# Letting branches into TensorE's queue only between half jobs of a hybrid decoder layer

## The chip, the cores and the metric

The kernel runs on one core of one Trainium2 chip. The metric is the device time of one execution in microseconds (us). A profiled execution of the same kernel gives the trace. Its engines are TensorE (PE: matrix products, weight loads shown apart as PEld), VectorE (DVE), ScalarE (ACT), GpSimd (POOL) and SyncE (SP, which issues the transfers).

## The reference

One layer over 1024 tokens of width 1024, everything float32. The input is normalised and multiplied by one wide matrix; its columns feed three branches, their gates and a merge.

```python
h = rms_norm(x, norm_g[l])
proj = jnp.einsum('bsd,dn->bsn', h, w_in[l])
(a_val, a_glu, a_gate, b_q, b_f, b_i, b_gate,
 c_q, c_k, c_v, c_gate, c_f, merge) = jnp.split(proj, split_points, axis=-1)
ya = conformer_conv(a_val, a_glu, ...) * jax.nn.silu(a_gate)
yb = hgrn2(b_q, b_f, b_i, ...) * jax.nn.silu(b_gate)
yc = forgetting_attention(c_q, c_k, c_v, c_f + fox_f_bias[l], ...) * jax.nn.silu(c_gate)
branches = jnp.stack([ya, yb, yc], axis=2)
branch_d = jnp.einsum('bskc,kcd->bskd', branches, w_branch[l])
gates = jax.nn.sigmoid(merge.reshape(B, S, N_BRANCH, D_MODEL))
mixed = jnp.sum(gates * branch_d, axis=2)
x = x + jnp.einsum('bsd,de->bse', mixed, w_out[l])
```

Branch a is a causal convolution of width 31 with a layer norm. Branch b is a gated linear recurrence with 8 heads of width 128 (hgrn). Branch c is causal attention with 16 heads of width 64, normalised q and k, and a forget bias.

## The kernel before

**The linear stream.** Every dense product is cut into jobs (138 of them): 128 output columns by 1024 tokens, in two half jobs of 512 tokens. To keep float32 accuracy, operands are split into a high and a low part, and a half job is 8 steps of k with three matmuls each (high x high, high x low, low x high), 24 matmuls of 128x512 into one PSUM bank. `lin` (L359) runs through the jobs in a fixed order. At the start of a job it fetches the weights of the job after next and splits the weights of the next one (`split`, L342): ScalarE copies the high part (whi, L354), VectorE subtracts it (wlo, L355). Raw, high and low weights have two buffers each, so the copy for a job needs the buffer of the job two before. When a half job is done, `j.done` evicts its bank.

**The branches** are generators that share the engines with the stream. Per head pair c (0 to 7) the jobs are q, k, v and gate of attention, then q, f, i and gate of hgrn. As their results come, these start:

- `qkprep` (L478): eight transposes of k (L494), ScalarE squares; two pairs of matmuls with the matrix ones_bd give the mean squares of q, one bank per half (L501). Then Ln (L504, L507), Exp (L508, L510), Square (L516), and VectorE's Newton step that reads both banks (L519) before they are given back.
- `att` and `soft`: four groups of score blocks (Khi, Klo against Qst, one bank each, two ScalarE evictions each), maximum, Exp, sums, then products with V and the row sums with ones64, both with 64 output rows.
- `hgrn` (L711): levels of 2, 8 and 32 tokens. The inner levels are 32 small products with 32 output rows (`inner_level`), level 32 is 24 of them. Then seven transposes of k, seven products KN times V (L843), a chain of seven states, and 15 output products (L859).
- `conv`: 31 VectorE steps for a group of 128 channels, while the stream goes on.

**Who decides the order.** `Sched.run` (L169) holds an estimate of each engine's time. The stream is a generator too: only where it yields can a branch go on. There the run loop resumes each branch that is ready by its estimate, until none is left, and returns to the stream. Branches take their PSUM banks from a pool of five (`bget`, `bput`, L229, L235), the stream has three of its own.

```python
if pick is not None:
    if not self.resume(pick):
        self.cos.remove(pick)
    continue
if linlive and (self.lin.cond is None or self.lin.cond()):
    linlive = self.resume(self.lin)
    continue
```

What the generators issue is the program's order. The framework's scheduler then sets the final order of each engine by priority and by its own clock, and can pull an instruction past others. On the chip each engine's queue runs strictly in that order: a stalled matmul holds up everything behind it.

Of the kernel before, what the change touches and what calls it, by code (L numbers as in the profile page):

```python
# [198 lines left out]
def build(tc, x, norm_g, w_in, conv_w, conv_b, ln_g, ln_b, hgrn_g, f_bias, qn_g, kn_g,  # L199
# [24 lines left out]
    def ps_lin():  # L224

        lbanks.append(lbanks.pop(0))
        return lbanks[-1]
# [70 lines left out]
    def fput(*ts):  # L298
        F.put(*ts)
# [38 lines left out]
    def fetch(j):  # L338
        j.raw = wpool.tile([P, KT, P], F32, name="wraw", tag="wraw", bufs=2)
        nc.sync.dma_start(out=j.raw, in_=j.src.rearrange("(k p) c -> p k c", p=P))  # L340

    def split(j, eng=nc.vector, pin=lambda ins: ins):  # L342
        if j.narrow:
            j.buf = F.get(dt=F32R)
            j.hi = j.buf[:, 0:S].rearrange("p (k c) -> p k c", k=KT)

            pin(nc.scalar.activation(j.hi, j.raw, AF.Copy))
            pin(eng.tensor_tensor(out=j.hi[:, :, 32:48], in0=j.raw[:, :, 0:16],
                                  in1=j.hi[:, :, 0:16].bitcast(F32), op=ALU.subtract))
            return  # L350
        j.hi = wpool.tile([P, KT, P], F32R, name="whi", tag="whi", bufs=2)
        j.lo = wpool.tile([P, KT, P], F32R, name="wlo", tag="wlo", bufs=2)
        with tc.high_priority(0 if sc.lin is None else HP):
            pin(nc.scalar.activation(j.hi, j.raw, AF.Copy))  # L354
            pin(eng.tensor_tensor(out=j.lo, in0=j.raw, in1=j.hi.bitcast(F32), op=ALU.subtract))  # L355
        sc.t["act"] += 950
        sc.t["dve"] += 1240

    def lin(jobs, hooks):  # L359
        seq = [(0, 0), (1, 0), (2, 0), (0, 1), (1, 1), (2, 1)]  # L360
        seq += [(n, h) for n in range(3, len(jobs)) for h in (0, 1)]
        for m, (n, half) in enumerate(seq):
            j = jobs[n]
            for i in {3: (3,), 5: (4,)}.get(m, (n + 2,) if n > 2 and not half else ()):
                if i < len(jobs):
                    fetch(jobs[i])
            for i in {5: (3,)}.get(m, (n + 1,) if n > 2 and not half else ()):
                if i < len(jobs):
                    split(jobs[i])
            if not half and j.pre is not None:  # L370
                yield from j.pre()
            X = j.X()
            ps = ps_lin()
            hs = slice(half * H2, (half + 1) * H2)
            for k in range(KT):
                a, b = X[0][k][:, hs], X[1][k][:, hs]
                sc.mm(ps, j.hi[:, k, :], a, k == 0, False, 228)
                sc.mm(ps, j.hi[:, k, :], b, False, j.narrow and k == KT - 1, 228)
                if not j.narrow:
                    sc.mm(ps, j.lo[:, k, :], a, False, k == KT - 1, 228)  # L380
                if (m, k) in hooks:
                    hooks[m, k]()
                if k == 3:
                    yield 0
            j.done(half, hs, ps)
            if j.narrow and half:
                fput(j.buf)
            yield 0

        yield from odirect()  # L390
# [723 lines left out]
    def odirect():  # L1114
        yield lambda: od.get("ok")
        mh, ml = Y["mix"]
        parts = [(o, min(H2, OW - o)) for o in range(0, OW, H2)]
        for i in range(KT):
            yield need(2)
            xt, ot = F.get(), F.get()  # L1120
            ts_ = slice(i * P, (i + 1) * P)
            nc.sync.dma_start(out=xt[:, 0:OW], in_=x[ts_, OC * P:])
            pss = [ps_lin() for _ in parts]
            for k in range(KT):
                for a, b, first, last in ((mh, "hi", True, False), (mh, "lo", False, False),
                                          (ml, "hi", False, True)):
                    for ps, (o, n) in zip(pss, parts):
                        sc.mm(ps[:, 0:n], a[k][:, ts_], od[b][:, k, o:o + n], first and k == 0,
                              last and k == KT - 1, n * 0.42 + 3)
                if k in (3, 7):  # L1130
                    yield 0
            for ps, (o, n) in zip(pss, parts):
                sc.tt(ot[:, o:o + n], ps[:, 0:n], xt[:, o:o + n], ALU.add)
            nc.sync.dma_start(out=out[ts_, OC * P:], in_=ot[:, 0:OW])
            fput(xt, ot)
# [176 lines left out]

    sc.start(yb(), "yb")
    sc.run(lin(jobs, {(1, 7): lambda: x_two_out(0), (2, 3): lambda: x_two_out(1)}))
    ctx.close()
    return sc
# [29 lines left out]
```

## Time and profile before

| | |
|---|---|
| median of 3 runs | 1905.27 us (1904.55 to 1906.85) |
| profiled execution, its own time | 1904.65 us |
| its span, first to last instruction | 1902.9 us |
| mean granted clock of TensorE | 0.999 |
| busy: TensorE, VectorE, ScalarE, GpSimd | 1885.2, 1285.2, 953.6, 186.2 us |
| attention and hgrn on TensorE | from about 65 to 1062 us |
| linear stream alone on TensorE | from there on |

The profile gives busy time per engine, the groups of instructions, who waited for whom, and a timeline. Matmuls are pipelined, so rows overlap: the time that a matmul takes from the next one is the distance between their starts, not its own length. Rows that say x64 stand for 64 records in a row; a float32 product that is not of the split kind leaves two records (xcount 8 is four products). Time that an engine stood idle ahead of a row is in brackets, with what ended it.

### The profile page before, as it was taken

Reading aid. Unit: us, or ns where it says so; the run is one execution under the profiler, and the core shown is the slowest. Engines: PE = TensorE matmul, PEld = TensorE weight load, DVE = VectorE, ACT = ScalarE, POOL = GpSimd, SP = SyncE. Lnnn points to the kernel's source line nnn. Section 1 sums busy time; section 2 is a strip of 40 time slices with the busy share of each in tenths; the row PEclk is TensorE's granted clock in tenths of the full one; section 3 lists DMA queues with packets and bytes.
Section 4 is the critical chain, followed back from the end, with each engine's and each line's share of the span. In section 5 each row is a group of like instructions: output and inputs, shape, how many; then the busy total and the mean of one; then the engine's idle time right before and its main releaser. Section 6 shows DMA issues by size and latency. Waiting matters only on the chain.

```text
span 1902.9 us, 27032 instructions
## 1 busy us (share of the span) xinstructions
PE 1885.2 (99%) x11075; PEld 1548.8 (81%) x11075; DVE 1285.2 (68%) x1692; ACT 953.6 (50%) x1508; POOL 186.2 (10%) x164
## 2 busy tenths in 40 slices
PE   8999999999999999999999999999999999999999
PEld 6877878878878788787887888888888888888888
DVE  6567595775856857659577999999995467413431
ACT  6777768767687687776875411111221234321210
POOL 2021120211202111112021100000000010000000
PEclk9999999999999999999999999999999999999999
DMA  4111101111111111110111322222444553213431
GB/s 147 48 31 45 56 23 45 56 45 45 34 45 45 34 52 38 45 56 23 45 56 46 133 78 67 78 67 67 134 147 151 194 160 92 85 45 104 118 129 49
DMA packets 173011, 140.82 MB, mean 74 GB/s; under 512 B 4909, under 2 KB 155445, under 8 KB 172888
## 3 DMA queue, kind: packets, MB, share of 16 engines
q1 hardware_dynamic: 172888, 139.10, 23.7%
q8 instruction: 86, 1.41, 0.3%
q14 instruction: 37, 0.30, 0.1%
HBM read 109.72 MB, written 29.36 MB: 73 GB/s over the span
## 4 chain that ended last, share of the span: by engine, by line
PE 85%; ACT 7%; DVE 3%; DMA 3%; issue 1%; SPq 0%; POOL 0%; DVEq 0%; ACTq 0%; POOLq 0%
PE bank L111 84%; ACT fb L124 4%; ACT khi L124 1%; DVE fa L128 1%; PE bank L115 1%; ACT L124 1%; DMA zdram<-fa 1%; ACT fa L124 1%; DVE fb L128 1%; DMA fa<-zdram 1%; DMA fb<-in_hgrn_norm_g_dram 1%; DMA wraw<-in_w_in_dram 0%; ACT whi L354 0%; DVE klo L132 0%; DVE wlo L355 0%
## 5 line engine op out<-in xcount | busy, mean ns | idle before, releaser
L111 PE MATMUL bank<-hT_hi,whi 128*128 128x512 f32 x1792 | 706.8, 394 | 0.0
L111 PE MATMUL bank<-hT_hi,wlo 128*128 128x512 f32 x1792 | 701.3, 391 | 0.8 <-DVE wlo L355 0.8
L111 PE MATMUL bank<-hT_lo,whi 128*128 128x512 f32 x1792 | 701.2, 391 | 0.0
L111 PEld LDWEIGHTS bank<-hT_hi,wlo 128*128 128x128 f32 x1792 | 336.8, 188 | 72.9 <-issue 2.4
L111 PEld LDWEIGHTS bank<-hT_hi,whi 128*128 128x128 f32 x1792 | 337.0, 188 | 69.8 <-issue 3.2
L111 PEld LDWEIGHTS bank<-hT_lo,whi 128*128 128x128 f32 x1792 | 337.3, 188 | 63.8 <-issue 0.2
L354 ACT ACTIVATE whi<-wraw 128x1024 fp32r<-128x1024 f32 x137 | 144.9, 1058 | 356.9 <-PE bank L111 346.9
L132 DVE SCALAR_TENSOR_TENSOR fa<-fa,taps,fa 128x1024 f32<-128x1024 f32 x240 | 300.0, 1304 | 0.4
L355 DVE TENSOR_TENSOR wlo<-wraw,whi 128x1024 fp32r<-128x1024 f32 x137 | 191.8, 1400 | 112.2 <-ACT whi L354 109.9
L128 DVE TENSOR_TENSOR fa<-fa,fa 128x512 f32<-128x512 f32 (+3 forms) x226 | 173.8, 784 | 67.0 <-ACT fa L124 50.4
L124 ACT ACTIVATE fa<-bank 128x512 f32<-128x512 f32 (+2 forms) x182 | 102.5, 572 | 141.7 <-PE bank L111 131.0
L111 PE MATMUL bank<-yhi,whi 128*128 128x512 f32 x384 | 149.4, 389 | 0.0
L111 PE MATMUL bank<-yhi,wlo 128*128 128x512 f32 x384 | 149.2, 389 | 0.0
L111 PE MATMUL bank<-ylo,whi 128*128 128x512 f32 x384 | 149.2, 389 | 0.0
L124 ACT ACTIVATE fb<-bank 128x512 f32<-128x512 f32 (+5 forms) x262 | 114.2, 451 | 40.6 <-PE bank L111 32.1
L128 DVE TENSOR_TENSOR fa<-fa,fb 128x512 f32<-128x512 f32 (+1 forms) x121 | 81.8, 676 | 59.0 <-ACT fb L124 37.8
L124 ACT ACTIVATE fb<-bank,negF,rk 128x256 f32<-128x256 f32 (+1 forms) x184 | 89.2, 549 | 47.7 <-PE bank L111 31.8
L124 ACT ACT_TABLE_LOAD x83 | 106.5, 1283 | 4.5 <-DVE fb L128 3.0
L132 DVE SCALAR_TENSOR_TENSOR fa<-fa,bank 128x512 f32<-128x512 f32 x96 | 65.7, 686 | 60.0 <-PE bank L111 60.0
L124 ACT ACTIVATE fa<-fa 128x256 f32<-128x256 f32 (+3 forms) x109 | 75.9, 721 | 55.3 <-DMA zdram<-fa 29.6
L124 ACT ACTIVATE fb<-fb 128x1024 f32<-128x1024 f32 (+2 forms) x96 | 88.1, 953 | 15.8 <-DVE fb L128 14.8
L111 PEld LDWEIGHTS bank<-yhi,wlo 128*128 128x128 f32 x384 | 72.1, 188 | 15.0
(163 smaller groups left out, 2128.7 us busy)
## 6 DMA issues: line engine op xcount, KB each, us to landing
wraw<-in_w_in_dram SPq DMA_DIRECT2D x113, 512.0 KB, 3.8
wraw<-in_w_branch_dram SPq DMA_DIRECT2D x24, 512.0 KB, 3.9
zdram<-fa SPq DMA_DIRECT2D x16, 512.0 KB, 4.1
mdram<-fa SPq DMA_DIRECT2D x32, 256.0 KB, 2.0
fa<-mdram SPq DMA_DIRECT2D x16, 512.0 KB, 3.8
fa<-zdram SPq DMA_DIRECT2D x16, 512.0 KB, 3.3
fa<-in_x_dram SPq DMA_DIRECT2D x9, 512.0 KB, 5.2
yc<-fb SPq DMA_DIRECT2D x8, 512.0 KB, 2.6
```

The costliest lines, as they stand in the source:

```text
L111: self.nc.tensor.matmul(out, lhsT=lhsT, rhs=rhs, start=start, stop=stop)
L115: self.nc.tensor.transpose(out, in_, ident)
L124: return self.nc.scalar.activation(out, in_, func, **kw)
L128: self.nc.vector.tensor_tensor(out=out, in0=a, in1=b, op=op)
L132: self.nc.vector.scalar_tensor_tensor(out=out, in0=a, scalar=s, in1=b, op0=op0, op1=op1)
L354: pin(nc.scalar.activation(j.hi, j.raw, AF.Copy))
L355: pin(eng.tensor_tensor(out=j.lo, in0=j.raw, in1=j.hi.bitcast(F32), op=ALU.subtract))
```

## The change

`lin` yielded twice in each half job: after the k step 3, that is 12 matmuls, and after the half job is evicted. The first of the two is removed. The two hooks of the start-up, the fetches and the splits stay where they are.

```diff
                     sc.mm(ps, j.lo[:, k, :], a, False, k == KT - 1, 228)
                 if (m, k) in hooks:
                     hooks[m, k]()
-                if k == 3:
-                    yield 0
             j.done(half, hs, ps)
             if j.narrow and half:
                 fput(j.buf)
```

No instruction is added or taken away, so what changes is their order. The rows below are instructions in the order of one engine's queue: line, operation, output <- inputs, shape, xcount. A name like bank4_80 or fa1_154_4395 is a buffer, number and use. Lines behind the removed ones are two lower after the change.

First place: TensorE in the middle of the fifth head pair (c = 4), where attention's last row sums (ones64, 64 output rows) meet an inner level of hgrn (gt0, 32 output rows). Linear matmuls are those with hT. Before:

```order
L111 MATMUL bank2_78<-hT_lo_144,whi_4463 128x512
L111 MATMUL bank5_81<-fa3_147_4258,ones64_86 64x256 x2
L111 MATMUL bank3_79<-fa6_149_4384,fb1_127_3800 64x256 x2
L111 MATMUL bank3_79<-fa6_149_4384,fb1_127_3800 64x128 x2
L111 MATMUL bank2_78<-hT_hi_143,wlo_4464 128x512
L111 MATMUL bank3_79<-fa4_150_4385,ones64_86 64x256 x2
L111 MATMUL bank4_80<-gt0_133,fa9_138_4045 32x48 x32
L111 MATMUL bank2_78<-hT_hi_143,whi_4463 128x512
```

After the change:

```order
L111 MATMUL bank2_78<-hT_hi_143,wlo_4454 128x512
L111 MATMUL bank5_81<-fa9_147_4271,ones64_86 64x256 x2
L111 MATMUL bank4_80<-gt0_133,fa1_138_4033 32x48
L111 MATMUL bank3_79<-fa0_149_4398,fb3_127_3786 64x256 x2
L111 MATMUL bank3_79<-fa0_149_4398,fb3_127_3786 64x128 x2
L111 MATMUL bank4_80<-gt0_133,fa1_138_4033 32x48 x4
L111 MATMUL bank3_79<-fa5_150_4399,ones64_86 64x256 x2
L111 MATMUL bank4_80<-gt0_133,fa1_138_4033 32x48 x27
L111 MATMUL bank0_76<-hT_hi_143,whi_4453 128x512
```

Two groups have become one, with the two kinds of small products interleaved.

Second place: TensorE a little later in the same pair. bank7 before and bank4 after hold the mean square of q's first half (ones_bd). Before, from the first ones_bd to the next use of that bank:

```order
L115 MATMUL bank3_79<-ident_84,fb1_158_4646 128x128 x4
L111 MATMUL bank4_80<-fb0_144_4243,fa1_154_4395 128x128 x2
L111 MATMUL bank7_83<-fb2_159_4804,ones_bd_101 128x512 x2
L111 MATMUL bank4_80<-fb0_144_4243,fa1_154_4395 128x128
...
L111 MATMUL bank1_77<-hT_hi_143,wlo_4763 128x512
L111 MATMUL bank7_83<-fb5_151_4392,fb0_144_4243 128x128
```

After the change, with 10 of the linear matmuls between the first two rows shown, 20 between the two groups of outputs and 3 ahead of the last products left out in part:

```order
L111 MATMUL bank4_80<-fb4_159_4766,ones_bd_101 128x512 x2
...
L111 MATMUL bank2_78<-hT_hi_143,wlo_4643 128x512
L111 MATMUL bank6_82<-fb5_144_4243,fa4_154_4409 128x128 x4
...
L111 MATMUL bank5_81<-fb0_160_4769,ones_bd_101 128x512 x2
...
L115 MATMUL bank6_82<-ident_84,fb4_161_4850 128x128 x4
L111 MATMUL bank1_77<-hT_hi_143,whi_4762 128x512
L111 MATMUL bank1_77<-hT_lo_144,whi_4762 128x512
L111 MATMUL bank1_77<-hT_hi_143,wlo_4763 128x512
L111 MATMUL bank4_80<-fb5_144_4243,fa4_154_4409 128x128 x3
```

KN times V (fb5, fa4) was 4, 2 and 1 products ahead of and around the first ones_bd; now four come after it, and the last three use its bank again.

Third place: ScalarE over the same stretch. fb1_158 before and fb6_158 after hold k, then the Ln of q's mean square. Before:

```order
L124 ACTIVATE fb1_158_4646<-bank3_79 128x512
L124 ACT_TABLE_LOAD
L124 ACTIVATE sm_119<-sm_119,eps_t_93 128x16
L124 ACTIVATE fb1_158_4646<-bank7_83,eps_t_93 128x512
L124 ACT_TABLE_LOAD
L124 ACTIVATE rk_118<-sm_119 128x16
L354 ACTIVATE whi_4918<-wraw_4760 128x1024
L124 ACT_TABLE_LOAD
L124 ACTIVATE fb1_158_4646<-bank3_79,eps_t_93 128x512
```

After the change:

```order
L124 ACTIVATE fb6_158_4646<-bank5_81 128x512
L354 ACTIVATE whi_4918<-wraw_4760 128x1024
L124 ACT_TABLE_LOAD
L124 ACTIVATE sm_119<-sm_119,eps_t_93 128x16
L124 ACTIVATE fb6_158_4646<-bank4_80,eps_t_93 128x512
L124 ACTIVATE fb4_161_4850<-bank2_78 128x512
L124 ACTIVATE fa2_152_4407<-bank6_82 128x128
L124 ACT_TABLE_LOAD
L124 ACTIVATE rk_118<-sm_119 128x16
L124 ACT_TABLE_LOAD
L124 ACTIVATE fb6_158_4646<-bank5_81,eps_t_93 128x512
```

The weight copy whi has moved from behind the first half's Ln to ahead of the table load for it.

## Rows read from the trace of the kernel before

**Rows 1.** The page's first part, the whole span: busy us (share) xinstructions.
```profile
PE 1885.2 (99%) x11075; PEld 1548.8 (81%) x11075; DVE 1285.2 (68%) x1692; ACT 953.6 (50%) x1508; POOL 186.2 (10%) x164
```
**Rows 2.** Timeline of TensorE from 560 us: start us, us, instruction.
```profile
560.98 0.62 PE L111 MATMUL bank<-fb,ones_bd 128*128 128x512 f32 x2
561.45 0.40 PE L111 MATMUL bank<-hT_hi,wlo 128*128 128x512 f32 x1
...
564.19 0.39 PE L111 MATMUL bank<-hT_hi,wlo 128*128 128x512 f32 x1
...
570.51 0.38 PE L111 MATMUL bank<-fb,fb 128*128 128x128 f32 x2
...
572.29 0.60 PE L115 MATMUL bank<-ident,fb 128*128 128x128 f32 x4
572.65 0.48 PE L111 MATMUL bank<-hT_hi,whi 128*128 128x512 f32 x1
```
**Rows 3.** Timeline of TensorE at 634 us: row sums alone between linear matmuls.
```profile
633.85 0.39 PE L111 MATMUL bank<-hT_hi,wlo 128*128 128x512 f32 x1
634.17 0.65 PE L111 MATMUL bank<-fa,ones 128*64 128x256 f32 x4
...
635.09 0.39 PE L111 MATMUL bank<-hT_lo,whi 128*128 128x512 f32 x1
```
**Rows 4.** Timeline of TensorE at 519 us: an inner level alone.
```profile
518.65 0.39 PE L111 MATMUL bank<-hT_hi,wlo 128*128 128x512 f32 x1
518.97 0.89 PE L111 MATMUL bank<-gt,fa 128*32 128x48 f32 x64
...
520.13 0.40 PE L111 MATMUL bank<-hT_lo,whi 128*128 128x512 f32 x1
```
**Rows 5.** Timeline of TensorE at 534 us: row sums and an inner level together.
```profile
533.78 0.50 PE L111 MATMUL bank<-hT_hi,wlo 128*128 128x512 f32 x1
534.22 0.65 PE L111 MATMUL bank<-fa,ones 128*64 128x256 f32 x4
534.80 0.89 PE L111 MATMUL bank<-gt,fa 128*32 128x48 f32 x64
...
535.95 0.40 PE L111 MATMUL bank<-hT_lo,whi 128*128 128x512 f32 x1
```
**Rows 6.** Timeline of TensorE at 553 us: KN times V, transposes of k.
```profile
552.17 0.40 PE L111 MATMUL bank<-hT_hi,whi 128*128 128x512 f32 x1
552.83 1.16 PE L111 MATMUL bank<-fb,fa 128*128 128x128 f32 x8 [0.26 <-ACT fa L124]
...
554.98 0.40 PE L111 MATMUL bank<-hT_hi,whi 128*128 128x512 f32 x1
555.65 0.66 PE L115 MATMUL bank<-ident,fb 128*128 128x128 f32 x4 [0.28 <-ACT fb L124]
```
**Rows 7.** Waits, whole span: who waited for whom, us in total, times, longest.
```profile
ACT whi L354 <- PE bank L111: 346.9, 79, 9.8
```
**Rows 8.** Timeline of ScalarE from 559 us: qkprep's Ln and Exp, a weight copy.
```profile
559.44 0.31 ACT L124 ACTIVATE sm<-sm,eps_t 128x16 f32<-128x16 f32 x1 [0.52 <-DVE sm L497]
559.66 0.67 ACT L124 ACTIVATE fb<-bank,eps_t 128x512 f32<-128x512 f32 x1
560.34 1.28 ACT L124 ACT_TABLE_LOAD   x1
...
561.76 1.05 ACT L354 ACTIVATE whi<-wraw 128x1024 fp32r<-128x1024 f32 x1
562.83 1.28 ACT L124 ACT_TABLE_LOAD   x1
564.12 0.69 ACT L124 ACTIVATE fb<-bank,eps_t 128x512 f32<-128x512 f32 x1
...
566.61 2.15 ACT L124 ACTIVATE fb<-fb 128x1024 f32<-128x1024 f32 x2
```
**Rows 9.** Timeline of VectorE at 569 us: the Newton step reads the two banks.
```profile
568.79 1.29 DVE L132 SCALAR_TENSOR_TENSOR fb<-bank,fb 128x512 f32<-128x512 f32 x2 [4.73 <-ACT fb L124]
```

## The prediction

> **What bounds the kernel now.** I read the page's busy times first: TensorE works for 99% of the span, VectorE for 68%, ScalarE for half [rows 1]. So only three things can move the time: what TensorE's own instructions cost in another order, a stall of TensorE, and a stall that goes. The number of matmuls is the same in both kernels (9538, counted in the two orders of instructions).
>
> The timeline of TensorE comes next. A linear matmul follows the one ahead of it after 0.228 us (twelve of them between the two linear rows of 2.74 us [rows 2]), whatever its own row says of its length. A branch's group is therefore priced from the start of the linear matmul ahead of it to the start of the second one behind it, less two such steps. Four matmuls of the row sums (64-row outputs) alone: 1.24 - 0.46 = 0.78 us [rows 3]. 64 matmuls of an inner level (32-row outputs) alone: 1.48 - 0.46 = 1.02 us [rows 4]. Both in one group: 2.17 - 0.46 = 1.71 us, of which 0.12 us is a wait (its first matmul starts 0.44 us after the linear one, 0.32 us where the same group stood alone) [rows 3, 5]. So 1.59 us without the wait, and the fusion saved 0.78 + 1.02 - 1.59 = 0.21 us. Fused, the engine changes the height of its output tile three times (128 to 64 to 32 to 128) in place of four: **one change of tile height costs 0.21 us** of TensorE.
>
> The same timeline shows the stalls that repeat in each of the seven later head pairs: KN times V starts 0.66 us after the linear matmul ahead of it (0.43 us too late), the second four transposes of k 0.67 us (0.44 us too late) [rows 6], the row sums 0.12 us as above. That is 0.99 us per pair, and each ends with a ScalarE or VectorE row whose work began when a linear job ended.
>
> **What the change does.** It takes away the scheduler's chance to let branches in after the 12th matmul of a half job. Branches wait for the end of the half job, more of them are ready there, and they go in together. SyncE moves the same transfers and GpSimd does the same work; a transfer or a table step shifts by a fraction of a job (10.9 us), and the weights are prefetched a whole job ahead, so I cost that at nothing: the two weight buffers hide it. If they did not, VectorE's split of a weight tile would come late and TensorE would wait for it.
>
> *Tile heights.* Counted over TensorE's whole order, the height of the output changes 169 times before and 207 times after: 38 more, although the number of branch groups barely moves (240 and 238). The first place in the order shows how: five changes became seven, because inner-level matmuls and row sums that now enter together are interleaved. Per head pair 21 became 26. Cost: 38 x 0.21 = **+8.0 us**. From below nothing excludes that a change straight from 64 to 32 rows is cheaper in other mixes; from above the row gives 0.21 plus perhaps its 0.12 us wait. I take 0.21, a row of just this mixture.
>
> *Stalls that go.* In the new order KN times V comes 24 linear matmuls after the last of the transposes that it needs (2 before), the first transposes of k leave with level 32, and the second come 38 linear matmuls after k's end (31 before). The row sums lead a group 21 linear matmuls behind the one ahead of it (1 before). 7 x 0.99 = **-6.9 us**; the bounds are none of it and all of it, and I take all, since the distances grew by several us against waits below half a us.
>
> *A stall that comes.* The second and third place in the order show it. The last three KN-times-V products (L843) now go into the bank of the first half of q's mean square (bank4). Before, the next to use those banks were the outputs of chunks 4 to 7 (L859), later in the queue. The bank is free only when VectorE has read it for the Newton step (L519). VectorE there needs Square, Exp and Ln of ScalarE. Before, ScalarE loaded the Ln table and finished the first half's Ln ahead of the next weight copy (whi). Now the weight copy stands first in ScalarE's queue, and that copy waits until TensorE has finished the job two before it (its buffer is one of two; these copies wait for TensorE 79 times, 346.9 us in all [rows 7]).
>
> So both engines start at the same moment: the end of v's job. ScalarE's leg, from its rows of before [rows 8]: from the start of whi to VectorE's read 568.79 - 561.76 = 7.03 us; now behind whi come also a table load (1.29), the small Ln with the first half's Ln (560.34 - 559.44 = 0.90), and the load with rk (561.76 - 560.34 = 1.42). Sum 10.64 us, then half of VectorE's pair, 0.65 us [rows 9]: **11.3 us** until the bank is free. Two short copies that also moved into this leg I leave out; they would add 0.1 or 0.2.
>
> TensorE's leg over the same stretch, in the order of the change: four products at 0.22 (eight of them in 1.78 us), 4 linear, the two matmuls of ones_bd (0.47), 20 linear, three products, eight transposes (four in 0.36), 3 linear [rows 2]: 0.89 + 0.91 + 0.47 + 4.56 + 0.67 + 0.72 + 0.68 = **8.9 us**. TensorE arrives 2.4 us early and stalls, with every linear matmul queued behind it: linear jobs, whose inputs are ready, cannot pass. The pattern stands in each pair from the second to the eighth: 7 x 2.4 = **+16.8 us**. Before, the same bank was free at about 569.4 (half of VectorE's pair) and used at 570.51: 1.1 us of slack [rows 2, 9], so no stall. Bounds: none, if ScalarE gets through 2.4 us sooner than its rows of before; 3.4 us, if each hand-over between the engines adds what the waits above show (0.4 us twice or so). I take 2.4.
>
> The Trainium skill (ScalarE: Activation LUTs, What ACT_TABLE_LOAD costs) counts 1.38 us of draining on top of each load, 2.66 us in all. The rows show none here: the load at 562.83 is followed by the next activation 1.29 us later [rows 8].
>
> *What else is late.* Five banks serve all branches; the attention's clusters of five blocks (now two in a row, 22 linear matmuls apart) need their banks evicted by ScalarE in between, 22 x 0.228 = 5.0 us. No row prices that; I take nothing and leave it to the third rival.
>
> Sum: 8.0 - 6.9 + 16.8 = +17.9 us on the profiled execution's 1904.65 us, so 1922.5 us. The median of the runs shown is 0.6 us above that execution; I leave the difference out. About 0.2% (3.8 us) is what a measurement of this kernel can tell from no change.
>
> **The rivals.**
> 1. The bank is free in time. Same switches, same stalls gone: 8.0 - 6.9 = +1.1, 1905.8 us, no change. It decides at ScalarE: if its leg is 8.9 us instead of 11.3, for instance because the weight copy starts sooner or a table load is missing. Against it: the new order still has all four loads in this leg, and the copy's buffer comes free only with the job's last use of it. Chance 0.10.
> 2. Faster: no bank stall, and the changes between 64 and 32 rows (30 of the 38 extra ones) cost nothing: 8 x 0.21 - 6.9 = -5.2, 1899.4 us. Against it: rows 5 is such a change, and it paid. Chance 0.05.
> 3. More stalls than one. The new order leaves more single linear matmuls between groups (38, before 23), places where the framework's scheduler thought a branch not ready yet. If three more of them per pair wait 0.43 us as KN did, 7 x 3 x 0.43 = +9.0: 1931.5 us. Chance 0.08.
> 4. Table loads with the skill's draining: four loads lengthen ScalarE's leg by an amount that no row shows. Chance 0.01.
>
> By the page's figure (an estimate from ScalarE: Activation LUTs of the Trainium skill) rival 4 would be 4 x 1.38 = 5.5 us more per pair, some 1961 us.
>
> **How the numbers follow.** The forecast has 0.76. Its own range is 1914 to 1930: the stall between 1.8 and 3.4 us per pair, the height change between 0.17 and 0.23 us. The range given reaches further down for a stall of half that size, up for rival 3: 1909 to 1933, which leaves rivals 1, 2 and 4 out (0.16). Slower: forecast and rivals 3 and 4, 0.85. Same: rival 1, 0.10. Faster: rival 2, 0.05.
>
> **What would show it.** Right: in each pair from the second a row of KN times V on TensorE with an idle time of about 2 us put down to VectorE's Newton step, seven such rows, and no more idle ahead of the transposes of k; TensorE's busy time a few us up. ScalarE's whi just ahead of the Ln load, ending within 1.2 us of v's last matmul. Wrong: that row without idle time (rival 1), idle time spread over many places of 0.3 to 0.5 us (rival 3), groups of mixed heights that are not longer than their parts less one change (rival 2). A stretch after the branches that got longer would mean that VectorE's later convolution steps, not the order of the branches, set the time; I expect none.

## The result, and the profile after

| | before | with the change |
|---|---|---|
| median | 1906.06 us (4 runs) | 1960.39 us (1960.32 to 1963.77, 4 runs) |
| ratio of the runs | | 1.0293, 95% interval 1.0281 to 1.0305 |
| profiled execution, its own time | 1904.65 us | 1963.77 us |
| mean granted clock | 0.999 | 0.990 |

Slower, as forecast, but by 54 us instead of 17.9, and outside the range. (The profiled execution is the slowest of the four, 3.4 us above the median; of before the profiled one stands 1.4 us under it. So sums over the two traces come to 59 us.)

The page's first part, where TensorE shows 22.8 us more busy time than in [rows 1], with the same number of matmuls:

```profile
PE 1908.0 (97%) x11075; PEld 1560.9 (80%) x11075; DVE 1264.0 (64%) x1692; ACT 953.7 (49%) x1508; POOL 212.5 (11%) x164
```

The waits of TensorE, whole span: who waited for whom, us in total, times, longest. Before, no row of this view but the start-up's was above 2.0 us.

```profile
PE bank L111 <- DVE fb L132: 17.0, 8, 2.4
PE bank L111 <- DVE fa L132: 9.4, 1, 9.4
PE bank L111 <- ACT fb L124: 6.3, 7, 1.0
PE bank L115 <- ACT fb L124: 5.8, 7, 4.6
```

Row one is the forecast stall; the other three were not in the forecast. And these waits add up to 38.5 us, not 59: something more is in the busy time.

**Where it is lost.** From the timelines of TensorE I took the start of the n-th matmul of the linear stream in each kernel and subtracted the same matmul's start of before. The stream is the same in all of them, so this lag shows in which stretch the time goes. n = 784 lies at the end of job 16, 3088 at the end of job 64. Jobs 1 to 16 are those of the first two head pairs, but the branches of a pair run while the next one's jobs stream. So the stretch up to 784 holds the first pair's branches and the first of the seven stalls; it is called the first pair below, and the 48 jobs behind it six pairs. 5400 to 5600 is where the stream turns to the jobs that need the layer norm.

```
lag behind the kernel before, us, at stream matmul n
                       150     784    3088    5400    5600
the change            -0.3     9.9    46.7    48.5    58.9
first pair as before  -0.8    -0.9    34.0    35.8    48.0
six pairs as before   -1.7     8.1     9.9    11.5    22.5
stream as before      -1.7     8.3    45.1    46.2    49.1
convolution ahead     -0.2     9.5    46.3    48.1    47.0
no Ln                  0.0     8.1    19.1    20.8    31.5
Exp held back         -1.6     6.2    17.2    19.0    30.0
level 32 on VectorE   -1.3     6.2    24.5    28.2    38.0
two mid entries       -0.5     4.7    22.7    28.1    27.1
Exp and convolution   -1.0     7.4    18.3    20.1    19.0
all three             -1.2     4.2     7.6    11.3    10.3
```

In the line of the change: 9.9 us in the first pair, 36.8 us in the next six (6.13 in each), 12.2 us in the stream. The start (n = 150) differs by up to 1.7 us from execution to execution whatever the kernel: in the trace of before TensorE itself stood at half clock for 3.4 us there, from 30.53 us on.

**The forecast stall** is there. Timeline of TensorE (start us, us, instruction, in brackets idle time and what ended it) in one pair; before, this place had four products (x8) with 0.26 us [rows 6]:

```profile
591.73 0.39 PE L111 MATMUL bank<-hT_hi,wlo 128*128 128x512 f32 x1
594.52 0.94 PE L111 MATMUL bank<-fb,fa 128*128 128x128 f32 x6 [2.40 <-DVE fb L132]
...
596.33 0.63 PE L111 MATMUL bank<-fb,fb 128*128 128x128 f32 x2
596.75 0.63 PE L111 MATMUL bank<-fa,fa 128*128 128x128 f32 x2
...
598.46 0.63 PE L111 MATMUL bank<-hT_lo,whi 128*128 128x512 f32 x1
598.89 0.43 PE L111 MATMUL bank<-hT_hi,wlo 128*128 128x512 f32 x1
599.16 0.40 PE L111 MATMUL bank<-hT_hi,whi 128*128 128x512 f32 x1
```

Seven such rows stand in the trace: 1.96 us once, 2.39 to 2.41 us six times. ScalarE's timeline of the same stretch has the order that the prediction read from the program, the weight copy ahead of the Ln and four table loads behind it (compare [rows 8]), and VectorE's Newton step ends it (compare [rows 9]):

```profile
582.85 1.06 ACT L354 ACTIVATE whi<-wraw 128x1024 fp32r<-128x1024 f32 x1 [1.38 <-PE bank L111]
583.92 1.28 ACT L124 ACT_TABLE_LOAD   x1
...
586.77 1.28 ACT L124 ACT_TABLE_LOAD   x1
588.07 0.22 ACT L124 ACTIVATE rk<-sm 128x16 f32<-128x16 f32 x1
588.30 1.28 ACT L124 ACT_TABLE_LOAD   x1
589.60 0.69 ACT L124 ACTIVATE fb<-bank,eps_t 128x512 f32<-128x512 f32 x1
590.30 1.28 ACT L124 ACT_TABLE_LOAD   x1
```

```profile
593.77 1.29 DVE L132 SCALAR_TENSOR_TENSOR fb<-bank,fb 128x512 f32<-128x512 f32 x2 [4.34 <-ACT fb L124]
```

From the start of whi to the Newton step: 593.77 - 582.85 = 10.92 us, against 10.64 in the prediction.

**What follows the stall** was not forecast: about 1 us after work is back, from 595.6 on, a product takes 0.42 us instead of 0.22 and a linear matmul 0.43 instead of 0.228, until 599. The windows view of that stretch (us, busy time of PE, PEld, DVE, ACT, POOL, the granted clock, DMA share, GB/s):

```profile
592.00:594.50 2.50, 0.12 (x1) 0.00 (x0) 0.73 (x2) 2.47 (x4) 0.00 (x0) 1.00 0.00 0
594.50:597.00 2.50, 2.48 (x16) 2.48 (x17) 2.43 (x3) 0.21 (x1) 0.00 (x0) 0.71 0.00 0
597.00:600.00 3.00, 3.00 (x13) 2.63 (x13) 2.90 (x6) 2.23 (x3) 0.00 (x0) 0.67 0.00 0
600.00:604.00 4.00, 4.00 (x24) 3.43 (x23) 3.11 (x4) 1.08 (x2) 0.00 (x0) 1.00 0.00 0
```

The clock is full through the idle 2.4 us and stands at its lower level (1.2 GHz) for 3.4 us once work is back. Cost: 0.29 x 2.5 + 0.33 x 3.0 = 1.7 us per stall, and it counts as busy time.

**A wait at ones_bd**, in six pairs, where before there was none ([rows 2] has the two matmuls without one). TensorE, then ScalarE:

```profile
574.83 0.55 PE L115 MATMUL bank<-ident,fa 128*128 128x128 f32 x3 [0.19 <-ACT fb L124]
...
576.83 0.73 PE L111 MATMUL bank<-fb,ones_bd 128*128 128x512 f32 x2 [0.99 <-ACT fb L124]
```

```profile
572.25 2.87 ACT L124 ACTIVATE fb<-bank 32x192 f32<-32x192 f32 x10
575.03 0.61 ACT L124 ACTIVATE fb<-fb 128x512 fp32r<-128x512 f32 x1
575.66 1.12 ACT L124 ACTIVATE fb<-bank 32x128 f32<-32x128 f32 x3
```

Branches that now enter together give ScalarE its small copies of level 32 in one clump; they end at 575.66 + 1.12 = 576.78, and the row of ones_bd starts 0.05 us later.

**The first pair** has the same clump at its worst, again with half the clock behind it (a linear matmul each 0.43 us until 178.7). TensorE, then ScalarE:

```profile
174.12 1.12 PE L115 MATMUL bank<-ident,fb 128*128 128x128 f32 x4 [4.60 <-ACT fb L124]
...
176.18 0.63 PE L111 MATMUL bank<-hT_lo,whi 128*128 128x512 f32 x1
```

```profile
172.40 4.10 ACT L124 ACTIVATE fb<-bank 32x192 f32<-32x192 f32 x13
```

**The stream behind the branches** loses 11.5 us in one place. TensorE, then VectorE:

```profile
1632.91 0.39 PE L111 MATMUL bank<-hT_lo,whi 128*128 128x512 f32 x1
...
1642.90 0.80 PE L111 MATMUL bank<-hT_hi,whi 128*128 128x512 f32 x1 [9.37 <-DVE fa L132]
1643.49 0.63 PE L111 MATMUL bank<-hT_lo,whi 128*128 128x512 f32 x1
```

```profile
1636.49 3.49 DVE L132 SCALAR_TENSOR_TENSOR fa<-fa,fa 128x1024 f32<-128x1024 f32 x3
...
1641.03 1.22 DVE L128 TENSOR_TENSOR ylo<-fa,yhi 128x1024 fp32r<-128x1024 f32 x1
1642.17 1.27 DVE L132 SCALAR_TENSOR_TENSOR fa<-fa,bank 128x512 f32<-128x512 f32 x2
```

The rest of the stream's 12.2 us is small: a new wait of 1.56 us near 1160 us for VectorE's split of a weight (the prediction's sign that the weight buffers do not hide it) adds 1.9 us, and an old one of 0.76 us near 1548 us is gone.

The stream's third bank is evicted by the row at 1642.17, and VectorE comes to it only then: ahead of it stands the work for the gated layer norm, which is late. SyncE's queue shows where it became late: the first load for the layer norm's statistics (L930) stands behind stores of the merged results (L1011), which wait for jobs of the stream, and leaves 67 us after the first sum over partitions starts (1497.55 us on GpSimd); before (last row, where the line is L932), 2 us after it (1472.39).

```profile
1558.84 5.76 SPq L1011 DMA_DIRECT2D mdram<-fa  x2
1564.65 0.43 SPq L930 DMA_DIRECT2D fa<-zdram  x1
...
1474.33 0.32 SPq L932 DMA_DIRECT2D fa<-zdram  x1
```

### The profile page after: what moved, and what is told of

Same layout as the page of the kernel before. It is cut to its first block, busy times and chain, and to the rows that moved or that the text cites. A ratio compares the mean times of both kernels' runs of the same rounds, so it can differ in the third digit from the quotient of the medians.

```text
span 1961.9 us, 26984 instructions
## 1 busy us (share of the span) xinstructions
PE 1908.0 (97%) x11075; PEld 1560.9 (80%) x11075; DVE 1264.0 (64%) x1692; ACT 953.7 (49%) x1508; POOL 212.5 (11%) x164
## 4 chain that ended last, share of the span: by engine, by line
PE 77%; ACT 11%; DVE 6%; issue 4%; DMA 1%; POOLq 0%; POOL 0%; SPq 0%; DVEq 0%; ACTq 0%
PE bank L111 77%; ACT fb L124 5%; ACT L124 3%; DVE fa L132 2%; DVE fa L128 2%; ACT khi L124 1%; PE bank L115 1%; ACT whi L354 1%; DVE wlo L355 1%; ACT fa L124 0%; DVE ylo L128 0%; DVE fb L132 0%; DMA fa<-in_x_dram 0%; POOLq L1339 0%; DVE fb L128 0%
## 5 line engine op out<-in xcount | busy, mean ns | idle before, releaser
L355 DVE TENSOR_TENSOR wlo<-wraw,whi 128x1024 fp32r<-128x1024 f32 x137 | 180.7, 1319 | 184.4 <-ACT whi L354 177.0
L128 DVE TENSOR_TENSOR fa<-fa,fa 128x512 f32<-128x512 f32 (+3 forms) x301 | 203.8, 701 | 44.9 <-DMA fa<-zdram 16.1
L124 ACT ACTIVATE fb<-bank 128x512 f32<-128x512 f32 (+5 forms) x292 | 129.6, 465 | 69.0 <-PE bank L111 40.0
L124 ACT ACTIVATE fa<-bank 128x512 f32<-128x512 f32 (+1 forms) x152 | 85.0, 567 | 144.8 <-PE bank L111 130.9
L124 ACT ACTIVATE fa<-fa 128x256 f32<-128x256 f32 (+2 forms) x121 | 89.3, 748 | 50.1 <-DMA zdram<-fa 25.9
L124 ACT ACTIVATE fa<-bank,negF,rk 128x256 f32<-128x256 f32 (+1 forms) x200 | 90.9, 545 | 44.0 <-PE bank L111 44.0
L635 POOL TENSOR_SCALAR_AFFINE_SELECT fa<-fa 128x256 f32<-128x256 f32 x64 | 65.3, 1022 | 355.7 <-ACT fa L124 355.7
L111 PEld LDWEIGHTS bank<-ylo,whi 128*128 128x128 f32 x384 | 72.1, 188 | 15.0
```

The lines of the kernel that those rows point to most:

```text
L111: self.nc.tensor.matmul(out, lhsT=lhsT, rhs=rhs, start=start, stop=stop)
L124: return self.nc.scalar.activation(out, in_, func, **kw)
L128: self.nc.vector.tensor_tensor(out=out, in0=a, in1=b, op=op)
L635: nc.gpsimd.affine_select(out=v, in_=v, pattern=[[0, 2], [1, P]], compare_op=ALU.is_ge, fill=NEG, base=0, channel_multiplier=-1)
```

## The experiments

My theory after the trace: (1) the bank stall is ScalarE's leg with its table loads, and it brings the clock down; (2) ScalarE's clump of level-32 copies makes the waits at ones_bd and in the first pair; (3) one entry per half job lets in too few convolution steps, so the layer norm's statistics stand further back in every queue. Rivals: one shift that everything else follows from; the 38 changes of tile height; small products rather than idle time as the reason for the clock.

### The entry put back, section by section

In each of three kernels the changed file gets the mid-job entry back for some of the 138 jobs:

```diff
                 if (m, k) in hooks:
                     hooks[m, k]()
+                if k == 3 and n < 17:
+                    yield 0
```

with `17 <= n < 65` in the second and `n >= 65` in the third.

> The mid-job entry is put back for the stream jobs 0 to 16 alone (the first head pair); everything behind runs as in the changed kernel. By the two traces TensorE is 9.9 us later at the 784th stream matmul than before the change, nearly all of it in one place of the first pair (transposes of the k gate that wait 4.60 us for ScalarE, then a stretch at half the clock). Theory A (each section of the program pays for its own missing entries): about 10 us off, 1950 us. Rival (the loss is made by what comes later, the first pair only hands on a shift): 1958 to 1961 us.

> The mid-job entry is put back for jobs 17 to 64 alone (the six later head pairs). Between the 784th and the 3088th stream matmul the changed kernel loses 36.8 us, 6.13 us in each pair: 2.40 us of bank stall as predicted, about 1.8 us of matmuls at half the clock right behind it, 1.9 us of new waits of the row-sum products and k transposes for ScalarE. Theory A: 37 us off, 1923 to 1925 us, and the mean granted clock back near 0.997. Rival (the tile-height changes, 38 more of them, make the pairs longer): they stay partly, 19 to 20 more than before with the entries back, so only about 4 us would go and the rest with the stalls, which cannot be told from A by the total; the profile must tell, by whether the 0.43 us matmuls go together with the 2.40 us stalls.

> The mid-job entry is put back from job 65 on (no attention work is left there; only VectorE's convolution, the layer norm's statistics and the preparation of the output still enter). Theory A: the 9.37 us stall of the first products for w_in of the gate, the 1.5 us stall near 1160 us and the half-clock stretch go: 12 us off, 1948 us; the layer norm's statistics are issued seven half jobs earlier again. Rival (the stall is owed to the pairs' delay, or to a DMA that came late): 1958 us or more.

Measured: first pair 1952.42 us (ratio to before 1.0247, interval 1.0231 to 1.0262), six pairs 1928.59 (1.0128, 1.0111 to 1.0145), stream 1953.42 (1.0252, 1.0236 to 1.0267); clocks 0.992, 0.995, 0.992. By the medians that is 8, 32 and 7 us off, 47 of the 54. The lags say the same place by place: with the first pair restored n = 784 stands at -0.9 us instead of 9.9; with the six pairs restored the lag grows by 1.8 us from 784 to 3088 instead of 36.8, and all of that in the first of them; with the stream restored the 11.5 us place is gone, but a new wait of 2.07 us for a weight's split near 1595 us takes some back. So each section pays for itself, and the rival of one common shift is out. (Medians are compared with the change's, from another chip, where the kernel before took 2 us more; theory A, read from the slowest execution, is a few us generous. Against the kernel before on their own chip the three gains are 5.9, 29.7 and 4.9 us, 40 of the 54; the gains by medians below shrink in the same way by 1 to 2 us.)

### The convolution's lead alone

TensorE's order stays as in the change, instruction by instruction; VectorE's convolution is let in further ahead of the planner's clock:

```diff
-                    if self.t["dve"] > pe + 1500 or c.ready > pe + 2000:
+                    if self.t["dve"] > pe + 4236 or c.ready > pe + 4736:
```

> The changed kernel with TensorE's order untouched (no entry put back); only the planner's lead for VectorE's convolution is widened, so that a single entry per half job lets in as many convolution steps as two did (limits of 1500 and 2000 ns raised by 2736 ns). The theory: one entry per half job lets in only one or two convolution steps of 1.23 us behind each eviction, so the convolution's last channel and with it the layer norm's statistics come later, and the first products that need them find the stream's bank not yet evicted. Theory A: as with the entries put back in this section, 11 to 12 us off, about 1948 to 1949 us. Rival (the stall comes from TensorE's own order, where a transfer or ScalarE ends the wait): 1958 to 1962 us. A third way: VectorE, holding convolution steps ahead of evictions, makes the stream wait for banks, 0.3 to 1.2 us at each of some 80 half jobs: 1965 us or more.

Measured: 1951.20 us (1.0243, 1.0228 to 1.0259), 9.2 us under the change by the medians, 12.0 between the profiled executions. The lag does not grow between 5400 and 5600 any more, and the waits of TensorE have lost just their row of 9.4 us. In SyncE's queue the statistics' first load is back 44 us earlier:

```profile
1514.89 5.76 SPq L1011 DMA_DIRECT2D mdram<-fa  x2
1520.71 0.42 SPq L930 DMA_DIRECT2D fa<-zdram  x1
```

The reason lies in the planner's rule, which can be followed in the code: each eviction of a half job sets VectorE's planned clock behind TensorE's, and a convolution step enters only while that clock is at most 1.5 us ahead. With one entry per half job, often only one or two steps go in where some four would fit (5.5 us of linear matmuls, 1.23 us a step). The planner, run for both, ends the convolution's last channel at job 109 before and at job 113 in the change, the first job that needs the layer norm; so all of the statistics are issued in one piece right ahead of it, behind stores of the jobs before. It is their place in the queue that is late, not the convolution: on the chip its last step starts behind the same part of the stream in all three traces (n = 4970 before, 4966 in the change and in this run), where the framework's scheduler has put it. The third way of the expectation (convolution steps that hold up evictions) does not show.

### ScalarE's table loads

First without Ln in that section (the normalized q and k have other values by it), then with the order Ln, Ln, Ln, Exp, Exp and the same output:

```diff
-        sc.act(u, kq, AF.Ln, scale=1.0 / 64, bias=eps_t)
+        sc.act(u, kq, AF.Ln, real=AF.Tanh, scale=1.0 / 64, bias=eps_t)
...
-            sc.act(y0[:, hs], pq[half], AF.Ln, bias=eps_t)
+            sc.act(y0[:, hs], pq[half], AF.Ln, real=AF.Tanh, bias=eps_t)
```

```diff
-            sc.act(y0[:, hs], pq[half], AF.Ln, bias=eps_t)
-        sc.act(r, u, AF.Exp, scale=-0.5)
+            last = sc.act(y0[:, hs], pq[half], AF.Ln, bias=eps_t)
+        tc.keep_in_program_order(last)
+        tc.keep_in_program_order(sc.act(r, u, AF.Exp, scale=-0.5))
```

(`real` is the function that is issued; the planner counts the first.)

> The changed kernel with the three Ln steps of q's and k's normalization done as Tanh, so that ScalarE's tables are not changed in that section (54 table loads instead of 84); the normalized q and k have other values by it. TensorE's and VectorE's instructions stand in the same order. Theory A (ScalarE's leg with its table loads ends the 2.40 us bank stall, and the stall is what brings TensorE's clock down behind it): the leg is some 4 us shorter, the seven stalls go, the 0.43 us matmuls behind them too; seven times 2.40 + 1.84 = 29.7 us off, 1929 to 1931 us, granted clock 0.995 or more. Rival B (the half clock is owed to the branch's small products, not to the wait): only 7 x 2.40 = 16.8 us off, 1943 us, the 0.43 us matmuls stay. Rival C (the stall comes from another wait): 1958 us or more.

> The changed kernel with k's small Exp held behind the second Ln of q on ScalarE, so that Ln, Ln, Ln, Exp, Exp run in this order: two table loads fewer in each pair (68 instead of 84), the same output. A load takes 1.28 us, so ScalarE's leg is 2.6 us shorter, just what the stall of 2.40 us needs. Theory A: the stalls and the half clock behind them go, as without Ln: 28 to 30 us off, 1930 to 1932 us. If a rest of the stall stays (0.1 to 0.5 us): the half clock should still go, 26 us off. Rival (a fixed cost of a wait on a bank, whatever its length): 1945 us or more.

Measured: 1936.07 us without Ln, 1936.00 us with Exp held back (both 1.0167, 1.0152 to 1.0182), clock 0.995 in both. That is 24.3 and 24.4 us off by the medians, and 27.5 and 29.2 between the profiled executions. In both, the lag grows by 1.83 us per pair instead of 6.13. The place in the second kernel, TensorE's timeline:

```profile
579.38 0.39 PE L111 MATMUL bank<-hT_hi,wlo 128*128 128x512 f32 x1
579.61 0.83 PE L111 MATMUL bank<-fb,fa 128*128 128x128 f32 x6
...
582.08 0.40 PE L111 MATMUL bank<-hT_lo,whi 128*128 128x512 f32 x1
582.31 0.39 PE L111 MATMUL bank<-hT_hi,wlo 128*128 128x512 f32 x1
```

No idle time, and no matmul at 0.43 us behind it, though the same small products run in the same order. So per pair 4.30 us hang on the stall: 2.40 of idle time and 1.9 behind it. Two table loads fewer (2.6 us) are enough. Rivals B and C of the first expectation are out: the clock falls with the wait, not with the small products. The medians are 4 to 5 us above what I expected, since the trace behind the expectation is of the slowest execution; by the lags at n = 5600 the gains are 27.4 and 28.9 us, near the expected 29.7.

### Level 32 on VectorE

```diff
-                            sc.act(Sv[a, ch:ch + 2, (j + 1) * m:P], pv[a, :, off:off + w], AF.Copy)
+                            sc.use("act", 0.833 * 2 * w + 100)
+                            nc.vector.tensor_copy(Sv[a, ch:ch + 2, (j + 1) * m:P], pv[a, :, off:off + w])
```

> The changed kernel with the level-32 copies out of the banks (24 per head pair, small) made by VectorE instead of ScalarE. Theory A (the 0.99 us wait of the row-sum products, the wait of the k transposes and the 4.60 us wait of the first pair all come from ScalarE's clump of small copies): 1.9 us off in each of six pairs and 5 to 8 us in the first, 16 to 19 us in all, 1941 to 1944 us; the seven bank stalls stay at 2.4 us. Rival (ScalarE's clump is late for other reasons, its table loads or the stream's own evictions, and VectorE's copies now hold up the klo and wlo steps): 1955 to 1965 us.

Measured: 1944.19 us (1.0213, 1.0196 to 1.0230). About the theory's total (0.2 us over its range), but not all by its route. The wait at ones_bd is gone from all six pairs. In the first pair 4.60 us became two waits, 1.25 us for the copies and 1.65 us for ScalarE, with half the clock behind them, so only 2.8 us are won there (from n = 150 to 784 the lag grows by 7.4 us instead of 10.2), less than the 5 to 8 expected. And the seven bank stalls did not stay at 2.4 us but came to 1.92 to 1.96, which gave an answer to another question. Two of them, from the windows view (one stall ends at 582.84, the other at 835.82; granted clock third from the end):

```profile
836.00:838.50 2.50, 2.50 (x18) 2.50 (x19) 2.40 (x4) 0.13 (x2) 0.00 (x0) 0.74 0.02 7
...
582.90:585.40 2.50, 2.50 (x21) 2.47 (x22) 2.40 (x3) 0.13 (x1) 0.00 (x0) 1.00 0.00 0
```

Six of the seven keep the full clock, one does not (the lag grows by 4.36 us in that pair, by 2.8 in each other). In the change itself the one stall of 1.96 us kept it too, and the six of 2.4 us lost it: with the clock at full speed a pair's growth of 2.8 us is little more than its 1.93 us of stall.

### Entries finer than before

```diff
-                if k == 3:
+                if k in (2, 5):
```

in the kernel before.

> The opposite direction: two entries in each half job (behind the 9th and the 18th matmul) beside the one at its end. The tile height changes 254 times, against 169 in the kernel before: by 0.21 us each 17.9 us more. Theory A (the price of a change holds, and with finer entries no stall is added): 1920 to 1924 us, mean granted clock 0.998 or more. Rival (a change of height costs nothing by itself, only stalls do): 1903 to 1907 us. Rival (finer entries bring stalls too): over 1930 us, with rows that show them.

Measured: 1930.97 us (1.0140, 1.0125 to 1.0155): the rival with stalls. Six us of it are one place in the stream, a wait for a weight's split with half the clock behind it:

```profile
1551.87 0.50 PE L111 MATMUL bank<-yhi,wlo 128*128 128x512 f32 x1 [3.84 <-DVE wlo L355]
```

The rest is small waits and the price of a change of height. Per pair the lag grows by 3.02 us, and TensorE's order there has 32 changes instead of 21, 11 more. Three waits of 0.57, 0.47 and 0.27 us are in it, each worth 0.2 us more than its bracket (0.26 in brackets was 0.43 too late in [rows 6]), 1.9 us in all, and the old 0.99 us are not: 3.02 + 0.99 - 1.9 = 2.1 us, 0.19 us a change. This is an estimate: it takes the old waits as all gone, and the order also holds 98 table loads instead of 84, which is not taken apart here.

### The single edits together

> The changed kernel with two of the single edits together: k's small Exp held behind q's second Ln, and the wider lead of the planner for VectorE's convolution. The theory of separate causes: the two gains add, 29 us of TensorE's time for the first and 12 us for the second off the profiled 1961.9 us, a span of 1920 to 1922 us, median 1921 to 1925 us. Rival (the two share a cause, as when either shift moves the layer norm's end): the sum is smaller by more than 4 us, 1928 us or more.

> The changed kernel with all three edits: k's Exp held back, the wider lead for the convolution, the level-32 copies on VectorE. Entries stay between half jobs only, and the height of TensorE's output tile still changes 207 times (169 before). If the stalls and the clock behind them were all that the prediction missed, what is left over the kernel before is the prediction's first two terms, +8.0 us for 38 changes of height and -6.9 us for old waits that are gone, and some rest of the first pair's wait (up to 3 us): 1906 to 1914 us, granted clock 0.998 or more. Rival (VectorE, with the copies and the convolution ahead of evictions, makes new stalls): 1918 us or more, with rows that show them.

Measured: 1923.38 us (1.0095, 1.0078 to 1.0112) for the first two edits, 1915.95 us (1.0056, 1.0041 to 1.0071) for all three, clocks 0.998 and 0.999. The first two add as separate causes should: 24.4 and 9.2 us of the medians make 33.6, and 37.0 were measured; by the lags at n = 5600, 28.9 and 11.9 make 40.8, and 39.9 were measured. With all three, 44 of the 54 us are gone though branches still enter only between half jobs. What is left of TensorE's waits that the change brought:

```profile
PE bank L115 <- DVE fb L818: 2.5, 6, 1.3
...
PE bank L111 <- ACT fb L124: 1.8, 2, 1.6
PE bank L111 <- DVE fa L132: 1.2, 2, 1.0
```

It is 2 us above the expected range. The lag has the places: 4.2 us in the first pair (1.25 and 1.64 us of wait, half the clock behind them), 2.7 us in the stream, and 0.57 us in each of six pairs. In the stream there is a wait of 1.03 us near 1345 us, which only the two kernels with the copies on VectorE have; three convolution steps stand ahead of the eviction there. Why is not shown: the copies themselves end at 1056 us. The 0.57 us in each pair is what the prediction's first two terms stand for: 0.57 + 0.99 of old waits gone - 0.45 for the one wait of 0.25 left = 1.1 us for 26 - 21 = 5 more changes, 0.22 us each.

## Why the prediction was wrong, point by point

- **Direction, and the bank stall: right**, in place, mechanism and size. ScalarE's leg 10.92 us against 10.64, seven stalls that sum to 16.4 us against 16.8; taking out table loads took out the stall. Rivals 1 and 2 fell with it.
- **Tile heights: right** within what the runs can tell, 0.19 and 0.22 us a change against 0.21. One reading under it was not: the 0.12 us of [rows 5] are no wait. The linear matmul ahead of that group is itself the first behind another small group, and such a one is followed after 0.34 us in [rows 3] and [rows 4] too (to 635.09 and 520.13 from the two rows below), not after 0.228. So 0.87 us of old waits a pair could go, not 0.99, and the two prices become 0.18 and 0.20 us.

```profile
634.75 0.50 PE L111 MATMUL bank<-hT_hi,whi 128*128 128x512 f32 x1
...
519.79 0.50 PE L111 MATMUL bank<-hT_hi,whi 128*128 128x512 f32 x1
```

- **Old waits that go: right** for the places named (no idle time at k's second transposes or at the first KN products), but the sum added no others. "What else is late" looked only at the attention's banks, and was answered with "No row prices that; I take nothing". **This step failed**: what was late next was ScalarE, with level 32's copies in one clump. Moving the copies took 1.25 us off each pair (1.82 to 0.57 us, with the other two edits in) and some 3 us off the first, where they stand behind a table load.
- **The stall was costed at its idle time alone: failed.** Behind each of six stand 1.7 (by the clock) to 1.9 us (by the lag) of half clock, 10 to 11 us in all, and some more in the first pair and behind the 9.4 us wait. So the 6.13 us of a pair are 2.40 of idle time, 1.9 behind it, 1.25 of the copies' waits and 0.57 for the heights less the old waits. The trace of before could have warned: its clock falls once while the stream runs, behind waits of 1.10 and 1.37 us at the start-up. No row read for the prediction covers that place, which would have put a bound from above beside the term: the same work at half speed for some us after each new stall.

```profile
30.50:34.00 3.50, 3.48 (x12) 2.37 (x11) 3.31 (x5) 2.02 (x4) 0.00 (x0) 0.51 0.06 13
```

- **Transfers and table steps "at nothing", and of VectorE's later convolution steps "I expect none": failed**, 11.5 us. The yield that was taken away serves VectorE's branches too. The prediction counted what it does to TensorE's order, where the stretch behind the branches hardly changes, and did not ask what a planner that enters half as often does to a coroutine that is admitted by a clock.
- **Rival 3** had the right kind (more waits than one) at too small a price: it took waits of 0.43 us, the size of those in the trace of before. **Rival 4's** 1961 us is the measured number by coincidence: its mechanism is refuted. The Trainium skill (ScalarE: Activation LUTs, What ACT_TABLE_LOAD costs) has 1.38 us of draining beside each load; in the trace the load at 588.30 takes 1.28 us and the next activation starts at 589.60, 0.02 us behind its end.

The lag at n = 5600, divided by place: first pair 9.9 less its share of the forecast (17.9 / 7 = 2.6), 7.4 us; six pairs 6 x (6.13 - 2.56) = 21.4; stream 12.2: 41 us, and with the forecast 17.9 that is the lag of 58.9.

Left open, and not tried: why the clock fell after one of seven nearly equal stalls of 1.9 us and not after the six others. In the first pair of the kernel with all three edits the lag still grows by 5.3 us (n = 150 to 784): 2.9 us are the two waits, 1.7 us the clock behind them (0.54 from 172.04 to 175.71), and the rest is not traced.

## What to carry to other kernels

When a scheduler loses entry points, ask of every kind of work that uses them, and not only of the bounding engine's order, what it now finds queued ahead of it: small copies arrive in clumps, and work admitted by a planned clock lands further back in a queue without any engine being busier. A stall of a matmul engine is to be priced with what its clock does afterwards; removing 2.4 us of idle time gave 4.3. And where a stall hangs on one leg of another engine, the order within that leg (here two table loads) is cheaper to mend than the order of the whole.

## What the runs showed of the hardware

TensorE's granted clock kept its upper level (2.4 GHz) after every single wait of 1.0 us amid the stream and after those of 1.56 to 1.67 us. It fell to the lower one (1.2 GHz) with each wait of 2.39 us and more there: behind the 2.4 us stalls for 3.4 us of work, 0.4 to 1.3 us after work was back; with waits of 4.6 and 9.4 us already during the wait, and for 4 to 5 us of work behind it (0.43 us for a linear matmul that otherwise takes 0.228).

Between these the length of the wait alone did not decide. 1.92 to 1.96 us left the clock up behind the first stall of four kernels and behind six of the seven of a fifth, and brought it down behind the seventh; 2.07 us in the stream brought it down. So did shorter waits close together: 1.25 and 1.65 us with 0.6 us of work between them (in both kernels with the copies on VectorE), and 1.10 and 1.37 us in the start-up of before. The clock's record begins 8 to 11 us into each execution; ahead of that, behind the wait of 2.5 us at the very start, a transpose took 0.21 us, and 0.11 us from there on.

The work done at the lower clock counts as busy time, so the view of waits showed 38.5 us where 59 were lost. A change of the output tile's height cost an estimated 0.18 to 0.22 us in three different orders.
